# A wider mask constant in a linear-attention kernel: every tile behind it moves by 1568 bytes of a partition

## The chip, the cores and the metric

The kernel runs on one core of one Trainium2 chip. The metric is the device time of one execution in microseconds (us). Before the change it is 128.49 us, the median of three runs (128.05, 128.49 and 130.7 us). One further execution was taken by the hardware profiler; it took 128.2 us and its span, from the first to the last instruction, is 126.4 us. All lines of profile below come from that execution, and times inside it count from the start of the span.

## The reference: what is computed

The inputs Q, K and V are fp32 arrays of batch 8, heads 12, sequence 512, dimension 64, 12.58 MB each. The output has the same shape and type.

```python
Q_feat = np.maximum(0, Q) + 1
K_feat = np.maximum(0, K) + 1
KV = np.einsum('bhkd,bhkv->bhdv', K_feat, V)
K_sum = np.sum(K_feat, axis=2)
numerator = np.einsum('bhqd,bhdv->bhqv', Q_feat, KV)
denominator = np.einsum('bhqd,bhd->bhq', Q_feat, K_sum)
out = numerator / (denominator[:, :, :, None] + 1e-10)
```

So each of the 96 heads needs one small 64x64 product of keys and values, and one product of its 512 queries with it. 37.75 MB are read and 12.58 MB are written.

## The kernel before, in words

**Layout.** The rows of the 96 heads are seen as (n, p, c): 128 partitions p, and c neighbouring rows of 64 numbers in a partition. For the inputs c is 32, so one n is 1 MB of fp32 in DRAM, 8 KB for each partition; for the output c is 8, so that one n is 2 KB for each partition. Work goes in 12 groups g of eight heads; two groups share one load of K, one of V and one of Q, and one output tile.

**Loads.** `load` (L102 to L117) and `load_q` (L119 to L124) issue DMAs on the GpSimd queue that turn fp32 into bf16 on the way: 8 KB of DRAM become 4 KB of a partition. A full load (L108, L121) brings two n: 8 KB of bf16 in each partition, 2.1 MB read, 1.05 MB written. The raw tiles `k_raw`, `v_raw` and `q_raw` have two buffers each (pool `in_pool`), so a load is issued when the buffer two loads back has been read. The first Q rows alone come as fp32 on the SyncE queue (L90) into a buffer of the output pool.

**Compute.** `k_features` and `q_features` (L151) make max(x, 0) + 1 on VectorE as max(x + 1, 1). `v_blocks` (L168 on VectorE, L170 on ScalarE) multiplies V by each of the four columns of a 0/1 constant, `mask`, so that one matmul (L192) forms keys times values of four heads at once. The constant is made once (L271) by summing blocks of the identity; it is also the column of ones that gives the sum of K (L280). `transposes` (L218, L221) turns the Q features; `out_matmuls` (L231) multiplies by the KV blocks; `norms` (L248, L249) divides and writes the fp32 output tile `o_sb`, 16 KB in each partition, five buffers (`out_pool`).

**Stores.** `store` (L131 to L148). Groups 0 to 9 go out on the GpSimd queue (L135), 1 MB each, as rows of 2 KB; group 10 (L140) and group 11 in five pieces (L143 to L148) on the SyncE queue. The main loop issues the first five stores behind the last load (L303 to L307), so that the output flows when the loads are done. The order of all work is written out by hand at the end of the kernel (L263 to L327).

**Where the tiles lie.** The pools are filled one after the other, each tile rounded up to 32 bytes. In a partition the first 16,384 bytes are set aside for the DMA descriptors, and then come, in bytes:

| tile | line | size in a partition | address before |
|---|---|---|---|
| four small constants, then `identity` | L70 | 128 + 256 | 16384 |
| `v_all` | L72 | 34816 | 16768 |
| `mask` | L73 | 16 (32 taken) | 51584 |
| `kva_all` | L74 | 4160 | 51616 |
| `k_raw`, two buffers | L105 | 2 x 8192 | 55776 |
| `v_raw`, two buffers | L105 | 2 x 8192 | 72160 |
| `q_raw`, two buffers | L94, L120 | 2 x 8192 | 88544 |
| `kf`, `qf`, `qt` | L157, L174, L213 | 36864 in all | 104928 |
| `o_sb`, five buffers | L88, L243 | 5 x 16384 | 141792 |

55776 is 217 x 256 + 224, and as all sizes behind it are multiples of 4096, every buffer from `k_raw` on lies 224 bytes past a multiple of 256.

Of the kernel before, what the change touches and what calls it, by code (L numbers as in the profile page):

```python
# [8 lines left out]
FP32 = mybir.dt.float32  # L9
# [10 lines left out]
def kernel(  # L20
# [18 lines left out]
    P = 128  # L39
# [19 lines left out]
    const = ctx.enter_context(tc.tile_pool(name="const", bufs=1))  # L59
# [10 lines left out]
    identity = const.tile([P, P], BF16, name="identity")  # L70
    NV = 4
    v_all = const.tile([P, 2, 2, C2, 4, DV], BF16, name="v_all")  # L72
    mask = const.tile([P, 4], FP32, name="mask")  # L73
    kva_all = const.tile([P, NV, 4, 2, D1], BF16, name="kva_all")  # L74
    kva_diag = [kva_all[:, i] for i in range(NV)]

# [281 lines left out]
```

## Time and profile before

| | before |
|---|---|
| median of three runs | 128.49 us |
| the profiled execution | 128.2 us |
| its span | 126.4 us |
| VectorE (DVE) busy | 82.7 us, 65% |
| TensorE (PE) busy | 68.5 us, 54% |
| ScalarE (ACT) busy | 67.8 us, 54% |
| GpSimd (POOL) busy | 24.6 us, 19% |
| DMA | 32.18 MB into their destinations, of which 19.6 MB are loads and 12.58 MB stores |

How to read it: the page counts the bytes of a DMA as they arrive. A load that turns fp32 into bf16 therefore shows half of the bytes that it reads. "DMA" in the 40 slices is the mean busy share of the core's 16 DMA engines, in tenths; in the tables of windows it can pass 1, since the records of neighbouring packets overlap a little. "GB/s" is the rate of all 16 together.

### The profile page before, as it was taken

Reading aid. Unit: us, or ns where it says so; the run is one execution under the profiler, and the core shown is the slowest. Engines: PE = TensorE matmul, PEld = TensorE weight load, DVE = VectorE, ACT = ScalarE, POOL = GpSimd, SP = SyncE. Lnnn points to the kernel's source line nnn. Section 1 sums busy time; section 2 is a strip of 40 time slices with the busy share of each in tenths; the row PEclk is TensorE's granted clock in tenths of the full one; section 3 lists DMA queues with packets and bytes.
Section 4 is the critical chain, followed back from the end, with each engine's and each line's share of the span. In section 5 each row is a group of like instructions: output and inputs, shape, how many; then the busy total and the mean of one; then the engine's idle time right before and its main releaser. Section 6 shows DMA issues by size and latency. Waiting matters only on the chain.

```text
span 126.4 us, 3095 instructions
## 1 busy us (share of the span) xinstructions
PE 68.5 (54%) x1344; PEld 58.1 (46%) x1344; DVE 82.7 (65%) x186; ACT 67.8 (54%) x72; POOL 24.6 (19%) x52
## 2 busy tenths in 40 slices
PE   0000299369369673566739757394844799574000
PEld 0000298369259462555629546283832577442000
DVE  0466642205597895999699695999649998298000
ACT  0006702980941999569890598919989526500000
POOL 6990020040002040020501009621022000200000
PEclk9999999958977999999995899999999559955555
DMA  3999999999999999999999999999999999999991
GB/s 98 325 216 214 213 213 215 215 213 216 215 211 218 215 210 216 218 213 211 220 209 215 218 211 215 218 211 216 242 407 415 424 407 390 384 380 386 384 313 51
DMA packets 8902, 32.18 MB, mean 255 GB/s; under 512 B 568, under 2 KB 824, under 8 KB 8760
## 3 DMA queue, kind: packets, MB, share of 16 engines
q0 software_dynamic: 7520, 28.84, 93.3%
q1 hardware_dynamic: 1368, 3.15, 7.0%
q8 instruction: 10, 0.16, 0.5%
q14 instruction: 4, 0.03, 0.1%
HBM read 37.75 MB, written 12.58 MB: 398 GB/s over the span
## 4 chain that ended last, share of the span: by engine, by line
ACT 37%; PE 34%; DVE 10%; DMA 7%; issue 3%; POOL 1%; ACTq 0%; DVEq 0%; POOLq 0%
PE kva_ps L192 29%; ACT v_all L170 24%; ACT qt L221 8%; DMA v_raw<-in_V_dram 7%; DVE o_sb L249 7%; ACT kva_all L205 4%; PE qt_ps L218 4%; DVE v_all L168 2%; DVE recip L248 1%; ACT L170 1%; DVE qt L221 1%; PE o_ps L231 1%; POOL k_raw L111 1%; ACTq L353 0%; ACTq L170 0%
## 5 line engine op out<-in xcount | busy, mean ns | idle before, releaser
L192 PE MATMUL kva_ps<-v_all,kf 64*64 64x272 bf16 x768 | 36.6, 324 | 25.9 <-ACT v_all L170 24.4
L192 PEld LDWEIGHTS <-kf 64*64 64x64 bf16 x768 | 33.1, 126 | 27.4 <-DVE v_all L168 14.0
L170 ACT ACTIVATE v_all<-v_raw,mask 128x1024 bf16<-128x1024 bf16 (+1 forms) x24 | 36.4, 1572 | 0.1
L221 ACT COPY qt<-qt_ps 128x1024 bf16<-128x1024 bf16 x23 | 22.2, 1017 | 25.4 <-PE qt_ps L218 25.4
L249 DVE TENSOR_TENSOR o_sb<-o_ps,recip 128x512 f32<-128x512 f32 x48 | 33.2, 692 | 1.7
L231 PE MATMUL o_ps<-kva_all,qt 128*64 128x130 bf16 x384 | 19.1, 233 | 19.9 <-DVE recip L248 7.6
L168 DVE TENSOR_SCALAR v_all<-v_raw,mask 128x2048 bf16<-128x2048 bf16 (+1 forms) x36 | 22.9, 691 | 8.6 <-DMA v_raw<-in_V_dram 8.6
L231 PEld LDWEIGHTS <-qt 128*64 128x64 bf16 x384 | 13.3, 114 | 26.1 <-DVE o_sb L249 10.6
L248 DVE RECIPROCAL recip<-o_ps 128x8 f32<-128x8 f32 x48 | 9.5, 199 | 13.6 <-PE o_ps L231 13.6
L218 PE MATMUL qt_ps<-identity,qf 128*128 128x128 bf16 x192 | 14.0, 228 | 1.2 <-ACT qt L221 1.0
L218 PEld LDWEIGHTS <-qf 128*128 128x128 bf16 x192 | 11.7, 102 | 3.7 <-issue 2.8
L205 ACT CAST kva_all<-kva_ps 64x260 bf16<-64x260 f32 x24 | 9.0, 374 | 6.2 <-PE kva_ps L192 5.9
L151 DVE TENSOR_SCALAR kf<-k_raw 128x1024 bf16<-128x1024 bf16 x24 | 9.1, 421 | 4.7 <-DMA k_raw<-in_K_dram 4.7
L135 POOL DMA_DIRECT2D out_dram<-o_sb x10 | 7.5, 764 | 23.6 <-DVE o_sb L249 15.0
L108 POOL DMA_DIRECT2D k_raw<-in_K_dram x5 | 3.6, 727 | 32.5 <-DVE kf L151 32.5
L108 POOL DMA_DIRECT2D v_raw<-in_V_dram x5 | 4.0, 792 | 26.7 <-ACT v_all L170 26.7
L151 DVE TENSOR_SCALAR qf<-q_raw 128x1024 bf16<-128x1024 bf16 x22 | 8.1, 428 | 0.0
L170 ACT ACT_TABLE_LOAD x1 | 1.3, 1283 | 10.5 <-DMA v_raw<-in_V_dram 10.5
L121 POOL DMA_DIRECT2D q_raw<-in_Q_dram x5 | 3.6, 721 | 0.0
L271 DVE TENSOR_REDUCE mask<-identity 128x4 f32<-128x128 bf16 x1 | 0.3, 286 | 4.7 <-POOL identity masks.py:199 4.7
L285 POOL MEMSET kva_all<- 128x130 bf16 x16 | 2.4, 196 | 0.0
L280 DVE CAST v_all<-mask 128x128 bf16<-128x128 f32 x2 | 2.2, 1639 | 0.0
(12 smaller groups left out, 7.2 us busy)
## 6 DMA issues: line engine op xcount, KB each, us to landing
out_dram<-o_sb POOLq DMA_DIRECT2D x10, 1024.0 KB, 21.1
k_raw<-in_K_dram POOLq DMA_DIRECT2D x5, 1024.0 KB, 14.3
v_raw<-in_V_dram POOLq DMA_DIRECT2D x5, 1024.0 KB, 13.0
q_raw<-in_Q_dram POOLq DMA_DIRECT2D x5, 1024.0 KB, 16.5
o_sb<-in_Q_dram SPq DMA_DIRECT2D x1, 1024.0 KB, 4.8
k_raw<-in_K_dram POOLq DMA_DIRECT2D x2, 512.0 KB, 9.5
v_raw<-in_V_dram POOLq DMA_DIRECT2D x2, 512.0 KB, 11.4
out_dram<-o_sb SPq DMA_DIRECT2D x1, 1024.0 KB, 8.6
```

Source lines behind the costliest of these rows:

```text
L108: nc.gpsimd.dma_start(out=t, in_=drams[x][:, 2 * s : 2 * s + 2])
L135: nc.gpsimd.dma_start(out=o_to[:, g % 2 : 2 * NP : 2], in_=outs[s][:, g % 2 : 2 * NP : 2], single_packet=True)
L151: nc.vector.tensor_scalar(out=dst, in0=src, scalar1=1.0, scalar2=1.0, op0=ALU.add, op1=ALU.max)
L168: nc.vector.tensor_scalar_mul(block[:, 0:cut], v_raw[:, 0:cut], mask[:, b : b + 1])
L170: nc.scalar.mul(out=block[:, cut:], in_=v_raw[:, cut:], mul=mask[:, b : b + 1])
L192: nc.tensor.matmul(halves[h][64 * eight : 64 * eight + 64, 0 : 4 * DV], lhsT=kf[ps, c, n, :], rhs=v_all[ps, g % 2, n, c], start=first, sto ...
L205: nc.scalar.copy(out=kva[ps, :, n, :], in_=halves[h][ps, 0 : 4 * DV].rearrange("p (b x) -> p b x", b=4)[:, :, 0:D1],)
L218: nc.tensor.transpose(qt_ps[:, c, r], qf[:, r, 2 * half + c, :, :], identity)
L221: copy(out=qts[g // 2][:, lo : lo + 2], in_=qt_ps.rearrange("p c r q -> p c q r"))
L231: nc.tensor.matmul(ops[c // 4][64 * j : 64 * j + 64, c // 2 % 2, (c % 2) * W : (c % 2) * W + W], lhsT=qt[:, c, q : q + 16, :], rhs=kva[:, ...
L248: nc.vector.reciprocal(out=recip, in_=cells[:, :, :, :, D:D1])
L249: nc.vector.tensor_tensor(out=o_sb[:, 2 * h + g % 2 : 2 * NP : NP, 4 * i : 4 * i + 4].rearrange("p n (b c) d -> p b c n d", b=2), in0=cell ...
```

## The change

The constant is allocated as a row of 396 fp32 numbers (1584 bytes) in place of 4 (16 bytes), and the kernel goes on with its first four columns.

```diff
     identity = const.tile([P, P], BF16, name="identity")
     NV = 4
     v_all = const.tile([P, 2, 2, C2, 4, DV], BF16, name="v_all")
-    mask = const.tile([P, 4], FP32, name="mask")
+
+    mask_row = const.tile([P, 396], FP32, name="mask")
+    mask = mask_row[:, 0:4]
     kva_all = const.tile([P, NV, 4, 2, D1], BF16, name="kva_all")
     kva_diag = [kva_all[:, i] for i in range(NV)]
```

`mask` and what lies ahead of it stay where they are. `kva_all` and everything behind it move up by 1568 bytes (1584 less the 16 that rounding had left free): `kva_all` to 53184, `k_raw` to 57344, `v_raw` to 73728, `q_raw` to 90112, `kf`, `qf` and `qt` to 106496 and on, `o_sb` to 143360. 57344 is 7 x 8192 and 143360 is 35 x 4096, so the three raw tiles lie at multiples of 8 KB and the output tiles at multiples of 4 KB. The last byte is 225280 in place of 223712. The instructions of each engine and of each queue, their shapes and their order are the same; line numbers of the changed kernel are higher by two from L74 on.

## The prediction

> **What bounds the kernel now.** I read the page first, then the waits, and then a table of windows over the two stages that the page's slices show.
>
> ```profile
> PE 68.5 (54%) x1344; PEld 58.1 (46%) x1344; DVE 82.7 (65%) x186; ACT 67.8 (54%) x72; POOL 24.6 (19%) x52
> ...
> DMA  3999999999999999999999999999999999999991
> GB/s 98 325 216 214 213 213 215 215 213 216 215 211 218 215 210 216 218 213 211 220 209 215 218 211 215 218 211 216 242 407 415 424 407 390 384 380 386 384 313 51
> ```
>
> No compute engine is busy for more than 65% of the span, but the 16 DMA engines are busy in every slice from the second to the last but one. There are two plateaus: about 214 GB/s while loads run, to about 91 us, and 380 to 424 GB/s while stores run. The kernel is bound by DMA throughout. The chain of waits (ACT 37%, PE 34%) goes through compute, but it is a chain of work that runs inside the time that the DMA engines need anyway; the next lines show the room.
>
> ```profile
> k_raw<-in_K_dram POOLq DMA_DIRECT2D x5, 1024.0 KB, 14.3
> v_raw<-in_V_dram POOLq DMA_DIRECT2D x5, 1024.0 KB, 13.0
> q_raw<-in_Q_dram POOLq DMA_DIRECT2D x5, 1024.0 KB, 16.5
> o_sb<-in_Q_dram SPq DMA_DIRECT2D x1, 1024.0 KB, 4.8
> ...
> out_dram<-o_sb SPq DMA_DIRECT2D x1, 192.0 KB, 6.1
> ```
>
> A load of 1.05 MB needs 1.05 MB / 214 GB/s = 4.9 us on the DMA engines, yet it lands 13.0 to 16.5 us after its issue: it stands in the queue for 8 us or more. Compute that frees a buffer up to some 8 us later costs nothing while loads run. At the end the room is smaller: the last 192 KB land 6.1 us after issue. The first Q load, on an empty queue, took 4.8 us, of which 1.05 MB at 380 to 424 GB/s are 2.5 to 2.8 us, so 2.0 to 2.3 us are latency. The last piece would take 2.0 to 2.3 plus 0.5 us, and so has about 3.4 us of queue ahead of it.
>
> ```profile
> 20.00:35.00 15.00, 9.61 (x141) 8.50 (x138) 4.47 (x11) 9.87 (x12) 1.43 (x2) 0.89 1.06 214
> 35.00:50.00 15.00, 9.96 (x218) 8.70 (x216) 12.28 (x29) 10.34 (x12) 2.14 (x3) 0.89 1.06 214
> 50.00:65.00 15.00, 9.36 (x232) 7.88 (x232) 13.59 (x32) 11.92 (x14) 2.43 (x3) 1.00 1.06 215
> 65.00:80.00 15.00, 10.19 (x216) 8.77 (x216) 12.25 (x29) 10.30 (x12) 4.73 (x7) 0.89 1.07 215
> ```
>
> ```profile
> 94.00:96.00 2.00, 0.84 (x16) 0.54 (x16) 1.93 (x6) 2.00 (x2) 0.00 (x0) 1.00 1.02 418
> 96.00:98.00 2.00, 0.84 (x16) 0.51 (x16) 1.97 (x4) 2.00 (x3) 0.75 (x1) 0.90 1.01 412
> 98.00:100.00 2.00, 1.18 (x24) 0.96 (x28) 2.00 (x5) 1.66 (x1) 0.00 (x0) 0.50 1.04 424
> 100.00:102.00 2.00, 2.00 (x43) 1.60 (x38) 2.00 (x6) 0.00 (x0) 0.00 (x0) 0.50 1.04 422
> 102.00:104.00 2.00, 2.00 (x26) 1.59 (x19) 1.93 (x6) 0.34 (x1) 0.00 (x0) 0.50 1.02 403
> 104.00:106.00 2.00, 1.74 (x32) 1.33 (x30) 1.56 (x4) 1.03 (x2) 0.00 (x0) 0.90 1.01 389
> ...
> 114.00:116.00 2.00, 1.29 (x16) 0.81 (x16) 1.90 (x7) 0.00 (x0) 0.00 (x0) 0.50 1.00 375
> 116.00:118.00 2.00, 0.00 (x0) 0.00 (x0) 0.57 (x1) 0.00 (x0) 0.00 (x0) 0.50 1.00 381
> 118.00:120.00 2.00, 0.00 (x0) 0.00 (x0) 0.00 (x0) 0.00 (x0) 0.00 (x0) 0.50 1.03 389
> ```
>
> The columns are the stretch, its length, busy us of PE, PEld, DVE, ACT and POOL with their instructions, the granted clock, the DMA share and the rate. The loads hold 214 to 215 GB/s of bf16, whatever the engines do beside them: 428 to 430 GB/s read from DRAM. The stores begin at 91.3 us (the window 90:92 shows 289 GB/s, a mixture of 64% at 214 and 36% at 420), run at 412 to 424 until 102 us, and at 365 to 403 (mean 387 over ten windows of 2 us) until 122 us. Every window has the same misaligned sources: all buffers of `o_sb` lie 224 bytes past a multiple of 256.
>
> **The change, part by part.** *The wider constant* adds no instruction. The reduce that fills it (0.3 us, once) and the three lines that read it have the shapes they had; only 1568 more bytes are reserved. Cost nothing.
>
> *Engine operands that move* (`kva_all`, `kf`, `qf`, `qt`, the raw tiles, `o_sb`). All were at multiples of 32 bytes and still are, so I take their durations as they are: L151 421 ns, L168 691, L170 1572, L221 1017, L249 692. This is not shown by a run; what covers it is the queue: 8 us for the loads, 3.4 us at the end. Were the 16 normalizations of L249 behind 90 us, 11.1 us in all, 10% slower or faster, that is 1.1 us, inside the cover. With the cover gone the end would move by this 1.1 us either way.
>
> *Loads.* 37.75 MB are read, and nearly all of it arrives as half the bytes. The misaligned side of a load takes 214 GB/s, while the stores drive the same misaligned side at up to 424. So the side that the change touches is used at half of what it is shown to bear, and the DRAM side, which gives 429 GB/s, is not touched. Value: 0. Bounds: the largest DMA rate of any window is 424 GB/s in the stores and 430 in the loads' reads, so loads could gain at most 430/428, 0.4 us of 86 us; on the other side the slowest load window, 5 to 20 us, has 213 in place of 214.5, 0.7% or 0.6 us.
>
> *Stores.* 12.58 MB, SBUF being read in rows of 2 KB. Here the misaligned side carries the full rate. Fast stretch (92 to 102 us): 406, 418, 412, 424, 422, mean 416 GB/s. Each DMA engine moves 424/16 = 26.5 GB/s there and 429/16 = 26.8 GB/s when it reads DRAM in the loads. A misaligned store thus comes within 1.2% of the best stream that any engine shows; there is no room for a large cost of misalignment in it. Slow stretch: about 8.16 MB leave after 102 us (12.58 less 10 us x 416 GB/s less 0.26 MB of the window 90:92), at 387 GB/s 21.1 us. What slows it isn't named by the trace. It persists at 381 to 389 GB/s after 116.6 us, when no engine computes, so it isn't contention with engines; and as alignment is the same in both stretches, alignment alone can't be what separates them. I take 0, by the nearest row, the stores at 424. Bounds: if aligned sources lift the slow stretch to 424, 21.1 becomes 8.16/424 = 19.2 us, a gain of 1.9 us; if they put the fast stretch down to 387, 4.16 MB take 10.7 in place of 10.0 us, and with 365, the slowest full window, for all 12.3 MB behind 92 us, 33.7 us in place of 31.1, a loss of 2.6 us at the far end; no stretch stays at 365, so I keep half of it, 1.3 us, for the range.
>
> A rule of the Trainium skill speaks for a gain. Its page "DMA: Bandwidth & Descriptors", section "How a descriptor splits into AXI transactions", says that a descriptor that doesn't start at a multiple of 256 bytes begins its first transaction at the boundary below, and the bytes ahead of the start cost beats of 32 bytes though unused. A row of 2 KB at 224 would cost 71 beats in place of 64. By the rule stores in the fast stretch would rise from 424 to 424 x 71/64 = 470 GB/s, a rate that no window shows, so the fast stretch doesn't bear it out there; on the slow stretch alone it would take 7/71 of 21.1 us, 2.1 us, and 387 would become 429, which is the rate that the loads read at. The trace agrees with the rule in the size of the slow stretch and disagrees in the fast one; by the rule's slow stretch the sum would be 126.1 us.
>
> **The sum.** 128.2 us of the profiled execution + 0 (constant) + 0 (operands) + 0 (loads) + 0 (stores) = 128.2 us. The median of the runs shown is 128.49, 0.3 us above the profiled one; I stay with 128.2.
>
> **The rivals.**
> *Stores speed up in the slow stretch.* For it: the slow rate, 387, is 9% below 424, a step that a fixed extra for each 2 KB row could make. Against it: five 1 MB stores ran at 416 with the same sources. Time: 128.2 - 1.9 = 126.3 us; to get past 2% below 128.49, 125.9 us, it needs 2.6 us, that is the fast stretch or the finish of the last pieces too. That last part exists: the issues at L147 and L148 take 1.1 to 1.2 us each at the end where L144 takes 0.34, and three such issues shortened by 0.8 us would add up to 2.4 us, if they wait for a full queue; the trace doesn't show what they wait for. So this rival reaches from 124.0 to 126.9 us.
>
> *Slower: aligned tiles collide.* With all raw and output buffers at multiples of 4 KB, a DMA write and an engine read in one partition agree in their low address bits, where before each tile had the same offset too, but the constants and `v_all` another one. If that made DMA packets wait, the place is the load stage with its 86 us. The price is 0.86 us for each per cent; it decides from 3% on (2.6 us, 214.5 falling below 208 GB/s), and 5% would give 128.2 + 4.3 = 132.5 us. For it: stores do have a slower mode that comes and goes with something unseen. Against: the load rate stays within 213 to 215 though DVE goes from 4.47 to 13.59 us busy in 15. The Trainium skill says in "SBUF — State Buffer", section "SBUF: two separate sides", that engine ports and DMA ports can't contend; the even load rate agrees.
>
> *The change doesn't do what it says*: excluded, since the addresses follow from the sizes of the tiles ahead of them.
>
> **How the numbers follow.** No change, 0.50: 127.5 to 129.3 us (0.4 us of the loads and the spread of the two lower runs to 128.05 below; 0.6 us and the 0.3 of the median above). Stores speed up, 0.32: 124.0 to 126.9 us, about 126.3 likeliest. Slower by collision, 0.18: from 130 to 132.5 us and on. The range from 125.4 to 129.8 takes in the first, most of the second, and the 1.3 us of slower stores above (129.5 and the 0.3 of the median); it leaves about 2 in 10 out. Two per cent, 125.9 and 131.1 us, is about what a measurement of this kernel can tell from no change, since its own three runs differ by that much. Of the second case some 0.12 lies within it, of the third 0.02: faster 0.20, within 0.64, slower 0.16.
>
> **What would show it.** Right: load windows at 214 to 215 GB/s again; store windows starting near 420 and falling to about 387 behind 102 us; durations of L249 (now L251) at 692 ns; the span within 1 us of 126.4. The stores' rival is right if the windows behind 102 us stand at 415 or more and the end comes 2 us sooner with the loads unchanged. The slower rival is right if load windows fall below 208. My prediction fails if the 428 GB/s of the loads isn't the limit of the DRAM side, or if the slow stretch comes from the 2 KB rows' alignment after all.

## The result and the profile after

The changed kernel takes 126.53 us, the median of four runs (126.34 to 126.8 us). Compared with the kernel before, its time is 0.987 of it, with a 95% interval of 0.984 to 0.990: 1.3% less, about 1.7 us. The profiled execution took 126.8 us with a span of 125.0 us, 1.4 us less than before. The change is within 2%, but the interval leaves out no change at all. Executions disturbed by a lower granted clock are left out of all ratios; the profiles of three experiments below (spans of 128.6 to 129.4 us) did fall into such executions, so there only the rates of windows are compared, and not spans.

First the page of the changed kernel, the lines that answer to the two plateaus:

```profile
PE 72.0 (58%) x1344; PEld 60.9 (49%) x1344; DVE 82.4 (66%) x186; ACT 67.8 (54%) x72; POOL 24.6 (20%) x52
...
DMA  3999999999999999999999999999999999999892
GB/s 86 339 214 210 219 211 216 214 211 219 211 215 215 216 212 215 215 218 214 211 218 214 211 221 208 215 215 215 216 372 414 413 418 418 409 415 413 337 372 101
```

The plateau of loads is where it was, at 214 GB/s. The plateau of stores no longer falls off: 409 to 418 GB/s, where before it went from 424 down to 380. The durations of engine instructions are those of before: L251 (L249 before) 692 ns, L172 1572 ns, L223 1016 ns. The windows of the changed kernel say the same with numbers (stretch, length, busy us of PE, of its weight loads PEld, of DVE, ACT and POOL, the granted clock as a share of TensorE's full clock, DMA share, GB/s):

```profile
35.00:50.00 15.00, 9.31 (x234) 7.82 (x232) 13.51 (x33) 11.86 (x13) 2.45 (x3) 1.00 1.06 214
50.00:65.00 15.00, 10.02 (x219) 8.70 (x215) 12.25 (x29) 10.30 (x12) 2.14 (x3) 0.89 1.06 215
```

```profile
98.00:100.00 2.00, 1.25 (x24) 0.80 (x21) 1.93 (x5) 2.00 (x2) 0.00 (x0) 0.87 1.03 420
100.00:102.00 2.00, 0.76 (x12) 0.40 (x8) 2.00 (x4) 2.00 (x3) 0.75 (x1) 0.50 1.03 420
102.00:104.00 2.00, 1.76 (x32) 1.44 (x36) 2.00 (x5) 1.08 (x1) 0.00 (x0) 0.50 1.03 420
104.00:106.00 2.00, 2.00 (x40) 1.28 (x32) 2.00 (x7) 0.00 (x0) 0.00 (x0) 0.50 1.03 414
...
114.00:116.00 2.00, 1.01 (x23) 0.52 (x17) 1.93 (x5) 0.00 (x0) 0.00 (x0) 1.00 1.00 406
116.00:118.00 2.00, 1.19 (x20) 0.79 (x22) 1.90 (x7) 0.00 (x0) 0.00 (x0) 0.63 0.78 311
118.00:120.00 2.00, 0.51 (x8) 0.27 (x6) 1.46 (x3) 0.00 (x0) 0.00 (x0) 0.50 1.05 408
```

Until 102 us both kernels store at the same rate (before 424 and 422 in the two windows ahead of 102 us, after 420 and 420). Behind it the kernel before drops to 403 and 389, and the changed one goes on at 420 and 414. One table over the whole stretch, first of before, then of after:

```profile
102.00:116.00 14.00, 10.48 (x188) 7.87 (x180) 10.91 (x27) 4.43 (x7) 0.75 (x1) 0.74 1.02 387
92.00:102.00 10.00, 5.58 (x111) 4.20 (x110) 8.48 (x19) 7.47 (x8) 1.50 (x2) 0.78 1.02 416
```

```profile
102.00:116.00 14.00, 10.76 (x216) 8.31 (x216) 11.46 (x27) 5.52 (x8) 0.75 (x1) 0.85 1.02 412
92.00:102.00 10.00, 5.81 (x128) 4.61 (x128) 6.90 (x16) 9.61 (x11) 1.51 (x2) 0.87 1.02 416
```

The last column is the reading: 416 and 416 in the fast stretch, 387 against 412 behind it. The 8.16 MB that leave behind 102 us take 21.1 us at 387 GB/s and 19.8 us at 412, which is 1.3 us of the 1.4 us between the spans. That is an estimate: it takes the rate of 102 to 116 us for all that follows, and so leaves out the gap that comes next.

New in this profile is the window 116:118 with a DMA share of 0.78: the DMA engines had all but caught up with compute. Of the 12.58 MB, about 10.2 had left by 116 us, and the ten stores issued until then hold 10.5; the next, that of group 10, was issued at 116.16 us (113.24 before). Whether that costs is asked by the last experiment.

### The profile page after: what moved, and what is told of

Its sections match the earlier page's. It is cut to its first block, busy times and chain, and to the rows that moved or that the text cites. A ratio compares the mean times of both kernels' runs of the same rounds, so it can differ in the third digit from the quotient of the medians.

```text
span 125.0 us, 3095 instructions
## 1 busy us (share of the span) xinstructions
PE 72.0 (58%) x1344; PEld 60.9 (49%) x1344; DVE 82.4 (66%) x186; ACT 67.8 (54%) x72; POOL 24.6 (20%) x52
## 3 DMA queue, kind: packets, MB, share of 16 engines
HBM read 37.75 MB, written 12.58 MB: 403 GB/s over the span
## 4 chain that ended last, share of the span: by engine, by line
ACT 37%; PE 33%; DVE 15%; DMA 7%; issue 3%; POOL 1%; ACTq 0%; POOLq 0%
PE kva_ps L194 28%; ACT v_all L172 24%; ACT qt L223 8%; DVE o_sb L251 7%; DMA v_raw<-in_V_dram 7%; ACT kva_all L207 4%; PE qt_ps L220 4%; DVE v_all L170 3%; DVE recip L250 2%; DVE qf L153 1%; ACT L172 1%; DVE qt L223 1%; PE o_ps L233 1%; DVE kf L153 1%; POOL k_raw L113 1%
## 5 line engine op out<-in xcount | busy, mean ns | idle before, releaser
L194 PE MATMUL kva_ps<-v_all,kf 64*64 64x272 bf16 x768 | 39.1, 340 | 25.4 <-ACT v_all L172 24.1
L194 PEld LDWEIGHTS <-kf 64*64 64x64 bf16 x768 | 35.2, 132 | 27.0 <-DVE v_all L170 13.9
L223 ACT COPY qt<-qt_ps 128x1024 bf16<-128x1024 bf16 x23 | 22.2, 1016 | 27.2 <-PE qt_ps L220 27.2
L172 ACT ACTIVATE v_all<-v_raw,mask 128x1024 bf16<-128x1024 bf16 (+1 forms) x24 | 36.4, 1572 | 0.1
L251 DVE TENSOR_TENSOR o_sb<-o_ps,recip 128x512 f32<-128x512 f32 x48 | 33.2, 692 | 1.6
L220 PE MATMUL qt_ps<-identity,qf 128*128 128x128 bf16 x192 | 14.8, 235 | 1.1 <-ACT qt L223 1.0
L220 PEld LDWEIGHTS <-qf 128*128 128x128 bf16 x192 | 12.4, 106 | 4.0 <-issue 3.1
L172 ACT ACT_TABLE_LOAD x1 | 1.3, 1283 | 10.5 <-DMA v_raw<-in_V_dram 10.5
```

What stands on the lines that cost most here:

```text
L172: nc.scalar.mul(out=block[:, cut:], in_=v_raw[:, cut:], mul=mask[:, b : b + 1])
L194: nc.tensor.matmul(halves[h][64 * eight : 64 * eight + 64, 0 : 4 * DV], lhsT=kf[ps, c, n, :], rhs=v_all[ps, g % 2, n, c], start=first, sto ...
L220: nc.tensor.transpose(qt_ps[:, c, r], qf[:, r, 2 * half + c, :, :], identity)
L223: copy(out=qts[g // 2][:, lo : lo + 2], in_=qt_ps.rearrange("p c r q -> p c q r"))
L251: nc.vector.tensor_tensor(out=o_sb[:, 2 * h + g % 2 : 2 * NP : NP, 4 * i : 4 * i + 4].rearrange("p n (b c) d -> p b c n d", b=2), in0=cell ...
```

## The experiments

The theory after the result (A) is that a store is slower when its rows of 2 KB don't start at a multiple of 256 bytes in SBUF. Its rivals: the raw tiles or the engines' operands matter (B), or the slow stretch comes and goes by chance (C).

**Only the output tiles aligned.** The kernel before, with 1568 bytes set aside just ahead of the output pool. The raw tiles stay 224 bytes past a multiple of 256. (The small `recip` tiles behind the output pool move along; no DMA reads or writes them.)

```diff
+    pad_pool = ctx.enter_context(tc.tile_pool(name="pad", bufs=1))
     out_pool = ctx.enter_context(tc.tile_pool(name="out_pool", bufs=OUT_BUFS))
...
+    pad_pool.tile([P, 392], FP32, name="pad")
```

> The output tiles alone are moved to a multiple of 4 KB; the raw tiles and all else stay where they were before. Theory A (a store whose rows of 2 KB start at a multiple of 256 bytes reads fewer bytes of SBUF): as the changed kernel, ratio 0.985 to 0.99, the store windows behind 102 us at 405 GB/s or more, loads at 214. Theory B (the raw tiles or engine operands matter): ratio 1.00, the windows behind 102 us at about 387. Theory C (the slow stretch comes and goes by chance): the rate of those windows need not follow the address at all.

The ratio to before is 0.986 (0.984 to 0.988), that of the whole change; it rests on two runs. Its windows (in this execution the stores began some 3 us later):

```profile
106.00:108.00 2.00, 2.00 (x38) 1.33 (x30) 2.00 (x7) 0.00 (x0) 0.00 (x0) 0.50 1.02 414
108.00:110.00 2.00, 2.00 (x28) 1.80 (x26) 1.52 (x4) 0.95 (x1) 0.00 (x0) 0.55 1.02 406
110.00:112.00 2.00, 1.74 (x40) 1.42 (x38) 1.97 (x4) 1.03 (x3) 0.00 (x0) 1.00 1.04 422
112.00:114.00 2.00, 1.84 (x64) 1.66 (x57) 0.85 (x3) 1.08 (x3) 0.75 (x1) 1.00 1.02 412
114.00:116.00 2.00, 0.64 (x16) 0.48 (x15) 0.82 (x3) 1.38 (x4) 0.00 (x0) 1.00 1.02 412
```

406 to 422 GB/s more than 10 us after the stores began: no slow stretch. The output tiles alone give the whole gain.

**All but the output tiles aligned.** The changed kernel with 224 bytes set aside ahead of the output pool in the same way (a pad of 56 numbers), which puts the output tiles back at 224 past a multiple of 256.

> Raw tiles, kva_all and the features lie as in the changed kernel, the output tiles again 224 bytes past a multiple of 256. Theory A: as before, ratio 1.00 and about 387 GB/s behind 102 us. Theory B: ratio 0.985 to 0.99 and 405 GB/s or more. Theory C: no relation.

The ratio is 1.002 (0.997 to 1.006). The slow stretch is back:

```profile
114.00:116.00 2.00, 1.04 (x32) 0.70 (x21) 0.26 (x2) 1.49 (x4) 0.49 (x1) 1.00 1.02 395
116.00:118.00 2.00, 0.88 (x16) 0.69 (x16) 1.93 (x5) 0.00 (x0) 0.00 (x0) 0.81 1.00 363
118.00:120.00 2.00, 1.47 (x20) 0.81 (x16) 1.93 (x6) 0.00 (x0) 0.00 (x0) 0.50 0.97 371
120.00:122.00 2.00, 1.29 (x16) 0.81 (x16) 1.90 (x7) 0.00 (x0) 0.00 (x0) 0.50 0.99 372
```

B falls, and with the two runs together C falls too: the rate follows the address of the output tiles. Where the loads arrive makes no difference that these runs can tell.

**Output tiles at 32 and at 128.** The changed kernel with 32, and with 128 bytes ahead of the output pool.

> As the changed kernel, but the output tiles 32 bytes past a multiple of 256. Theory A with unused beats (the bytes between the boundary and the start are read in vain: 1 beat of 32 bytes for each 2 KB here, 7 at 224): nearly as the changed kernel, 0.985 to 0.99, 400 GB/s or more behind 102 us. Theory A with one more transaction for each row, whatever its length (9 in place of 8): as slow as at 224, ratio 1.00 and about 387.

> As the changed kernel, but the output tiles 128 bytes past a multiple of 256. With unused beats (4 for each 2 KB): between the two, 387 x 71/68 = 404 GB/s behind 102 us, ratio about 0.99 to 0.995. With one more transaction for each row: as at 224, about 387, ratio 1.00.

At 32 the ratio to before is 1.000 (0.998 to 1.002), as slow as at 224; at 128 it is 0.997 (0.995 to 0.998), slightly better than at 224, and nothing like the 0.987 at 0. One line of the kernel with 32, to be held against the 422 GB/s that the kernel with aligned output tiles had in the same window above, and one of the kernel with 128, to be held against the 387 and 412:

```profile
110.00:112.00 2.00, 1.84 (x36) 1.36 (x38) 1.97 (x4) 1.25 (x2) 0.00 (x0) 1.00 1.01 393
```

```profile
102.00:116.00 14.00, 10.58 (x220) 8.26 (x218) 11.43 (x28) 5.14 (x8) 0.75 (x1) 0.87 1.02 393
```

If the price were that of the bytes read in vain, as the prediction counts them in units of 32 bytes ("beats"), it would be one for each row at an offset of 32, and seven at 224. The prices are the same, so it isn't them. A price for one more piece of each row, nine in place of eight, would fit 32 and 224, but no run shows the pieces, and that 128 is a little cheaper isn't explained by it.

**Stores alone.** These two kernels, and those of the next two parts, were each run once. All loads and all compute are left out; the output tiles are filled with ones and stored, from tiles at 224 and from tiles at 0.

```diff
+        for i in range(5):
+            t = out_pool.tile([P, 8, C, D], FP32, name="o_sb")
+            nc.vector.memset(t, 1.0)
+            outs.append(t)
+        for g in range(12):
+            s = g // 2
+            o_to = o_dram[:, 8 * s : 8 * s + 8]
+            nc.gpsimd.dma_start(
+                out=o_to[:, g % 2 : 8 : 2], in_=outs[(s + 4) % 5][:, g % 2 : 8 : 2], single_packet=True
+            )
```

> Leaves out all loads and all compute: five output tiles are filled with ones and the output is written from them, twelve stores of 1 MB one after the other on the GpSimd queue, with the rows of 2 KB that the kernel stores, from tiles 224 bytes past a multiple of 256. If the slow stretch needs the compute beside it or what the loads leave behind, all twelve run at 415 GB/s or more (30 us). If it belongs to the address and to the time or bytes since the stores began, about 420 for 10 to 12 us and then 380 to 390. If misalignment costs from the first row on, about 387 from the start (32.5 us).

> The same stores alone, from tiles at multiples of 4 KB: 415 GB/s or more in every window by every theory in which the address matters.

The windows of these kernels have the columns DVE and POOL, clock, DMA share and rate. First from 224, then from 0:

```profile
24.00:26.00 2.00, 0.00 (x0) 2.00 (x4) 1.00 1.03 371
...
38.00:40.00 2.00, 0.00 (x0) 0.00 (x0) 1.00 1.02 371
40.00:42.00 2.00, 0.00 (x0) 0.00 (x0) 1.00 1.01 367
```

```profile
24.00:26.00 2.00, 0.00 (x0) 2.00 (x4) 1.00 1.04 416
...
38.00:40.00 2.00, 0.00 (x0) 0.00 (x0) 1.00 1.03 408
40.00:42.00 2.00, 0.00 (x0) 0.00 (x0) 1.00 1.02 408
```

The spans are 60.4 and 57.6 us: 2.8 us for 12.58 MB. Without loads ahead, misaligned rows are slow from the first window on, and never reach 416. So neither compute nor the time since stores began makes the slow stretch; it is the fast one that has to be explained. In the kernel 8.16 of the 12.58 MB leave in the slow stretch, and 2.8 us x 8.16/12.58 = 1.8 us (an estimate), about the 1.7 us that the change is worth. The rate from 0 dips too, to 350 GB/s in the window 26:28, while GpSimd issues stores one after the other; that was not expected, and no run tests its cause.

**What makes the first stores fast.** Twice all of Q is loaded ahead of the same twelve stores from tiles at 224 (the loads of K and V and all compute are left out). In the first kernel the stores are issued while the loads run; in the second, one small copy makes them wait for the last load.

```diff
+        raw = in_pool.tile([P, 12, C4, D], BF16, name="q_raw")
+        for i in range(3):
+            nc.gpsimd.dma_start(out=raw[:, 4 * i : 4 * i + 4], in_=q_eights[:, 4 * i : 4 * i + 4])
...
+        nc.vector.tensor_copy(out=outs[4][:, 0, 0], in_=raw[:, 11, 0])
```

(The last line stands in the second kernel alone.)

> Leaves out the compute and the loads of K and V: all of Q is loaded (three loads, about 29 us), and the twelve stores of 1 MB from tiles 224 bytes past a multiple of 256 are queued behind it. If the fast first 10 us of stores in the kernel come from what stands ahead of them in the queue (stores issued long before they run), the first stores run at 415 GB/s or more here too and those issued while stores run fall to 370 to 390. If the loads ahead make no difference, 370 to 390 from the first window on, as in the run of stores alone.

> As the run that loads all of Q ahead of the stores, but one small copy from the last loaded tile into the first output tile makes the first store wait until the loads have landed, so that no store stands queued while loads run. If the fast first 10 us come from stores that were queued ahead, they are gone: 360 to 390 GB/s from the first window on. If they come from the loads themselves (the state in which they leave DRAM or the DMA engines), 415 GB/s or more for about 10 us again.

The first, in which seven stores were issued from 22.5 us on, well ahead of the end of the loads at about 33.5 us (the rate is 147 GB/s in the half microsecond ahead of it and 328 in the one behind):

```profile
22.52 5.23 POOL L76 DMA_DIRECT2D out_dram<-o_sb  x7 [18.87 <-DVE o_sb L68]
```

```profile
34.00:36.00 2.00, 0.00 (x0) 0.75 (x1) 1.00 1.03 424
36.00:38.00 2.00, 0.00 (x0) 0.75 (x1) 1.00 1.03 424
38.00:40.00 2.00, 0.00 (x0) 0.30 (x1) 1.00 1.03 424
...
44.00:46.00 2.00, 0.00 (x0) 0.75 (x1) 1.00 1.03 401
46.00:48.00 2.00, 0.00 (x0) 0.00 (x0) 1.00 1.02 391
48.00:50.00 2.00, 0.00 (x0) 0.00 (x0) 1.00 1.02 385
```

The second, in which the first store was issued at 34.26 us:

```profile
36.00:38.00 2.00, 0.00 (x0) 2.00 (x4) 1.00 1.00 352
38.00:40.00 2.00, 0.00 (x0) 2.00 (x4) 1.00 1.03 334
40.00:42.00 2.00, 0.00 (x0) 0.98 (x2) 1.00 0.99 350
42.00:44.00 2.00, 0.00 (x0) 0.75 (x1) 1.00 1.03 375
```

The fast 10 us are there with stores queued behind running loads, and gone without. So loads ahead are not enough: the stores must be issued while they run. Nor is standing in the queue enough, as the stores alone from 224 show:

```profile
22.54 6.83 POOL L72 DMA_DIRECT2D out_dram<-o_sb  x9 [22.09 <-DVEq L100]
```

Nine stores were issued by 29.4 us, and the last of them ran, by the bytes that had left, at about 47 to 50 us; they stood in the queue behind other stores for up to 17 us, and still ran at 367 to 383 GB/s. The fast stretch thus needs both, stores in the queue and loads that run ahead of them. It doesn't last for all that is queued: seven stores (7.3 MB) were, and some 10 us at 420 GB/s are 4.2 MB. Why it comes, and why it ends after 4 MB, no view of the profile shows; that stays open.

**Where the misalignment has to lie.** Stores alone again, but only 1792 of the 2048 bytes of each row are written. Three kernels: the source at 224 and the row in DRAM at 0; both at 224; the source at 0 (a tile at 32, from byte 224 of each row on) and DRAM at 224, all counted past a multiple of 256. The cut is that of the last two; the first takes the numbers 0:448 of each row.

```diff
+            rows = o_to[:, g % 2 : 8 : 2].rearrange("p n c d -> p n (c d)")
+            tile_rows = outs[(s + 4) % 5][:, g % 2 : 8 : 2].rearrange("p n c d -> p n (c d)")
+            nc.gpsimd.dma_start(out=rows[:, :, 56:504], in_=tile_rows[:, :, 56:504], single_packet=True)
```

> Stores alone again, but of each row of 2 KB only 1792 bytes are written (the rest of the output is left out): the source begins 224 bytes past a multiple of 256, the row in DRAM at a multiple of 256. Eight transactions in place of seven on the side of SBUF: slow, about 365 GB/s.

> As the run with a source at 224, but the piece written in DRAM begins at 224 too. If only the source's own start counts, about as slow as with the DRAM row at 0, 365 GB/s. If the price is that source and destination don't share their phase (pieces have to be cut twice), fast, 400 or more.

> The source begins at a multiple of 256, the piece written in DRAM at 224. If only the source counts, fast, 400 GB/s or more. If unequal phases count, or an unaligned start in DRAM counts by itself, 365 or less.

The spans are 56.8, 56.9 and 55.6 us; the mean of the nine windows from 34 to 52 us is 370, 368 and 376 GB/s. Equal offsets of source and destination don't help: that theory falls. With the row in DRAM at 224, an aligned source is still worth 1.3 us (56.9 against 55.6). This is also the only run here whose rows start at a multiple of 256 and of no larger power of two; in all others "aligned" means tiles at multiples of 4 KB. But 400 GB/s was expected of it and isn't reached, so either a misaligned start in DRAM has a price of its own or rows of 1792 bytes do; the run with both at 0, which would tell, was not made.

**A version meant to beat the change.** The changed kernel with the store of group 10 in two halves, each issued when its own normalizations are done.

```diff
-            nc.sync.dma_start(out=o_to[:, 0 : 2 * NP : 2], in_=outs[s][:, 0 : 2 * NP : 2])
+            nc.sync.dma_start(out=o_to[:, 0 : 2 * NP : NP], in_=outs[s][:, 0 : 2 * NP : NP])
+            nc.sync.dma_start(out=o_to[:, 2 : 2 * NP : NP], in_=outs[s][:, 2 : 2 * NP : NP])
```

> The changed kernel with the store of group 10 cut in two, each half issued as soon as its own normalizations are done. In the profile of the changed kernel the DMA engines run at 311 GB/s between 116 and 118 us, waiting for this store. If that gap costs in undisturbed executions too, 0.3 to 0.5 us less than the changed kernel: ratio to before 0.981 to 0.984. If it belonged to that one execution's lower clock, as the changed kernel, 0.985 to 0.988.

The median is 126.42 us, the ratio to before 0.986 (0.985 to 0.988): not to be told from the changed kernel, so it doesn't beat it.

```profile
116.00:118.00 2.00, 0.00 (x0) 0.00 (x0) 0.66 (x1) 0.00 (x0) 0.00 (x0) 0.50 1.03 410
```

There is no gap at 116 us here (share 1.03), and yet no gain. In this execution the last normalizations were nearly done by then (DVE 0.66 us in the window), where the profiled execution of the changed kernel was still busy with them (1.90 us). So the gap there goes with a compute chain that ran late in that execution. The kernel with 128 had its group 10 as late (store issued at 115.78 us). What the split does for such a late chain this profile doesn't show; over five runs it brings nothing.

## Why the prediction was right or wrong

The time, 126.53 us, lies in the range from 125.4 to 129.8, and the change lies within 2%, which had the largest chance. But the case put as likeliest, no change at 128.2 us, is not what happened. What happened is the first rival, "Stores speed up in the slow stretch", which had a chance of 0.32. The range held because it was drawn wide enough to take in most of that rival, and not because the sum was right: its mechanism was wrong for the stores. The prediction had named this as a way to fail, "if the slow stretch comes from the 2 KB rows' alignment after all", and that is what the runs show.

- *The constant, the engines' operands, the loads: 0.* Right. Load windows stand at 214 to 215 GB/s, the durations are the same, and aligning all but the output tiles gives 1.002. The argument, that the SBUF side of a load works at half the rate that stores reach, agrees with that; no run tests it by itself, and it compares a load's writing into SBUF with a store's reading from it.
- *The stores: 0, "by the nearest row, the stores at 424".* This is the step that failed. Measured: 412 in place of 387 GB/s behind 102 us, 1.3 us by the windows, and about 1.7 us by the ratio. The fault is in the choice of the row. It was true that "alignment alone can't be what separates" two stretches with the same alignment; it doesn't follow that alignment costs nothing in both. The fast stretch was an exception that comes only with stores queued while loads run, and it was taken for the rule. The runs of stores alone show the rule: 371 against 416 GB/s in the first window. The exception was also smaller than stated: 4.2 MB, about four stores and not five (in its sum, 0.7 us of the window 90:92 at 420 GB/s are 0.29 MB and not 0.26, which changes nothing).
- *The first rival's size, 1.9 us for 424 GB/s in the slow stretch.* A little large: it reached 412, and the span ended 1.4 us sooner, both a little short of the 415 GB/s and 2 us named as its signs. To get to 125.9 us it needed 2.3 us from 128.2; the 2.6 us counts from the median of 128.49. Its lower end, 124.0 us, hung on the last issues. Of those, L147 and L148 took 1.1 to 1.2 us each before; in the changed kernel they are shorter (two in 0.83 us, the last in 0.37 us), but the store of group 10 came later in that execution. With the split store, where there is no gap, the same two take 2.03 us with tiles just as aligned, so it is not the alignment that makes them short, and no run shows 2.4 us from it.
- *The slower rival.* Excluded by the load windows: 214 GB/s, far from the 208 at which it would have begun to count.
- *The rule on descriptors in the Trainium skill, "DMA: Bandwidth & Descriptors", section "How a descriptor splits into AXI transactions".* It gave 126.1 us by the slow stretch and was nearer than the sum. The trace agrees that a start off a multiple of 256 bytes costs a store, and about how much at 224. It does not agree with counting the unused bytes: by that an offset of 32 should cost a seventh of what 224 costs, and it costs the same (1.000).

## What to carry to other kernels

When a stage has a fast and a slow stretch with the same instructions, don't price an edit by the fast one: ask first which of the two is the rule, for which the operation alone, with nothing queued ahead, is the shortest test. Where stores bound the end, look at the address of the SBUF tile that they read. Here tiles at multiples of 4 KB were fast and tiles 32, 128 or 224 bytes past a multiple of 256 were slow; that a multiple of 256 is enough, only the run at 1792 bytes supports. Pools that are filled one after the other pass a small odd tile's offset on to all behind it, and 1.5 KB of padding ahead of the output pool alone was worth 1.4% here. An offset of 224 in the tiles that casting loads write cost nothing that could be measured.

## What the runs showed of the hardware that was not expected

- Misaligned stores of 2 KB rows run fast for some 10 us (416 to 424 GB/s in the run of loads and stores, 406 to 424 in the kernel before) if they were issued while earlier loads still ran. If not, they run at 324 to 389 GB/s in the full windows of the two runs without, also those that stood in the queue behind other stores.
- The price hardly depends on how far the source lies past the multiple of 256: the ratios to the kernel before, at 224, are 1.000 at 32, 0.997 at 128 and 0.986 to 0.987 at 0.
- Even aligned stores dipped, to 350 GB/s for 2 us, while GpSimd issued nine of them one behind the other; once issuing was over they reached 422. That the issuing is the cause is not shown.
